# A top-2-of-8 expert layer at the end of a two-layer trunk: another deal of the small experts' chunks, expert outputs gated as soon as they are whole, two finishes side by side, and other costs in the planner's clock

## The chip, the cores and the metric

One core of one Trainium2 chip. The metric is the device time of the whole kernel in microseconds (us), median of several runs. Engines are named as in the profile: PE (TensorE) for matmuls and transpositions, PEld its weight loads, DVE (VectorE), ACT (ScalarE), POOL (GpSimd), SP (SyncE), which here only issues DMAs.

## The reference

256 latent tokens and 256 context tokens of width 1024 go through two layers. Layer 0 has a mixer (gated MLP over chunks, windowed attention, state-space scan) and a dense SwiGLU; layer 1 has a mixer and eight SwiGLU experts of which each token uses two. All is float32. What the change touches most is the expert layer:

```python
def swiglu(h, wg, wu, wd):
    return (jax.nn.silu(h @ wg) * (h @ wu)) @ wd

def moe_ffn(h, w_r, wg, wu, wd):
    logits = (h @ w_r).astype(jnp.float32)
    top_v, top_i = lax.top_k(logits, TOP_K)
    gates = jax.nn.softmax(top_v, axis=-1)
    combine = jnp.sum(jax.nn.one_hot(top_i, N_EXPERTS, dtype=jnp.float32) * gates[..., None], axis=-2).astype(h.dtype)
    out = jnp.zeros_like(h)
    for e in range(N_EXPERTS):
        out = out + combine[..., e:e + 1] * swiglu(h, wg[e], wu[e], wd[e])
    return out
...
        x = x + mod[5] * f
```

Each expert has gate and up weights of 1024 x 2816 and a down weight of 2816 x 1024; `mod[5]` is a row of 1024 factors.

## The kernel before

**Two stages.** Up to about 890 us the kernel does both mixers, layer 0's dense SwiGLU and the router (called the first stage below). From there to the end it does the experts (the expert stage), in which every one of 264 weight tiles of 1 MB comes from HBM once, in an order fixed when the program is built, on SP's queue.

**Experts by rank.** The router ranks the experts by the number of their tokens. Ranks 0, 1 and 2 are "wide" (128 token slots; rank 0 has 32 more, the "rest", `NE` in the code, that use its weights too), ranks 3, 4 and 5 have 64 slots, ranks 6 and 7 have 32 (`CAPS`). An expert's work goes in 11 chunks of 256 hidden columns, three tiles each: two of gate and up, one of down. A wide chunk needs its weights split in a high and a low part: ACT copies (`whi`, L275), DVE subtracts (`wlo`, L276), and PE makes three products. Small chunks use the raw float32 tile (`wraw`) at once, in row and column tiles of the array (`tiled` L1561, `tiled_up`).

**Order of the expert stage.** `RUNS` (L1530) says which small chunks go beside which wide expert: a run is a wide expert's 11 rounds with so many 32-slot and 64-slot chunks dealt among them. Before: four 32-slot chunks, then expert 1 with 6 of 32 and 11 of 64 slots, expert 0 with 6 and 11, expert 2 with 4 and 11, and two 32-slot chunks last. A round of `experts` (L1600) is on PE: gate and up of the wide chunk (`gu`, 24 matmuls of 512 columns), down of the previous wide chunk (`py`, 12), for expert 0 the same for the rest (`gux`, `pyx`), then gate/up (`gu`) and down (`pys`) of the small chunks, and the transpositions of the hidden rows (`mTx`, `mT`). For 32 slots the transposition is a matmul by `sel`, a sum of two permutations, which also adds the two halves (`turn`); ACT and DVE then make `silx` (`turned`, L1592 on).

**Finishes.** When an expert's down sums stand complete in PSUM, `finishes` (L1755) runs it through `finish` (L1762): DVE multiplies by `mod5row` (`y`, L1774 and L1778; for 32 slots in four pieces of 32 rows), ACT and DVE split it in `yh` and `yl`, PE scatters it back to tokens with a one-hot matrix (`ohT`, from `onehot` L1500) into `sc`, and DVE adds it with the token's gate to `acc` (L1788). One finish runs at a time, and `y` is made only when the one-hot is there. The finish that comes last sends out eight DMAs of 128x256 (L1791). `finish` is a generator that gives way after each unit, so its matmuls lie among those of the chunks.

**What sets the order.** In the expert stage the instructions of PE and ACT are in the order in which the program wrote them. Which generator steps next, and when splits and loads are laid, goes by a planner's clock (`clk`): every matmul (`mm`, L366) and transposition (`tp`, L381) adds its assumed cost to it, and `PIECE`, `LANDS` and `SPLIT` are the assumed times of a tile on the queue and of a split. `Weights._due` lets a wide tile be split when the clock has passed the tile's landing and the last split:

```python
        if not net.routed:
            return net.o.clk - self.at[i] > net.LAG
        return net.o.clk > self.land[i] and net.o.clk > self.splits - net.SPLIT / 2
```

In the first stage the same clock times the splits (`LAG`) and the generators, and a list scheduler orders the engines' streams from there. Raw tiles live in 12 buffers in the expert stage; a load is issued when a buffer comes free.

Of the kernel before, what the change touches and what calls it, by code (L numbers as in the profile page):

```python
# [340 lines left out]
class Net:  # L341
# [1158 lines left out]
    def onehot(self, p):  # L1500

        nc = self.nc
        yield from until(lambda: len(self.ohT) < 2)
# [10 lines left out]
        ohT = self.mp.tile([P, 2, P], F32R, tag="ohT", name="ohT", bufs=2)  # L1514
# [5 lines left out]
    YB, YH = 1, 1  # L1520
    NRAW, MKRAW = 4, 5
    MPRAW, HL_B, LAG, NS = 3, 2, 6.0, 2
    PIECE, LANDS, SPLIT = 2.45, 4.8, 1.15
# [4 lines left out]
    RUNS = ((None, (4, 0)), (1, (6, 11)), (0, (6, 11)), (2, (4, 11)), (None, (2, 0)))  # L1528
# [32 lines left out]
    def tiled(self, ps, x, w, ws, a, z):  # L1561

        m = x.shape[-1]
        n = (ws.stop - ws.start) * m // P
        for g in range(P // m):
            self.mm(ps[m * g:m * g + m, :n], x, w[:, ws.start + n * g:ws.start + n * g + n], a, z)
            if g:
                self.o.clk -= 4 * n * 0.000422

    def tiled_up(self, ps, x, w, k):  # L1570

        for g in range(2):
# [3 lines left out]
            if g or k % 2:  # L1576
                self.o.clk -= 4 * 256 * 0.000422

    def narrow_mid(self, ps, m):
        v = self.mp.tile([P, 256], F32, tag=f"mid{m}", name="mid", bufs=2 if m == 32 else 1)  # L1580
# [3 lines left out]
    def turn(self, pt, at, v, m):  # L1584
        for j in range(2):
            b = v[:, P * j:P * j + P]
            if m == 32:
                self.mm(pt[:, at + 64 * j:at + 64 * j + 64], b, self.sel, True, True)
            else:
                self.tp(pt[:, at + P * j:at + P * j + P], b)  # L1590

    def turned(self, pt, at, m):  # L1592

        src = pt[:, at:at + 4 * m].rearrange("p (j g s) -> p j g s", j=2, g=2)
# [5 lines left out]
    def experts(self):  # L1600
# [6 lines left out]
        self.finishing = False  # L1607
        self.ndone = 0
        self.sel = self.mp.tile([P, 64], F32, name="sel", bufs=1)
        nc.vector.tensor_tensor(self.sel, self.c("ident", 0, 64), self.c("swap", 0, 64), op=ALU.add)  # L1610
        o.spawn(self.gather(0), 2)
        pw, pn = None, []
        for w, ns in self.rounds() + [(None, [])]:
# [71 lines left out]
            if mids:  # L1685
                pt, at = self.bank("mTx"), 0
                for *_, m, v in mids:
                    self.turn(pt, at, v, m)
                    at += 4 * m
            pw = None  # L1690
            if w:
                pm = self.bank("mT")
                for j in range(2):
                    self.tp(pm[:, P * j:P * j + P], sil[:, P * j:P * j + P])
                mh = self.mp.tile([P, 256], F32R, tag="mh", name="mh", bufs=1)
                ml = self.mp.tile([P, 256], F32R, tag="ml", name="ml", bufs=1)
                self.split(mh, ml, pm[:, :256])
                pw = [*w, mh, ml, None]
            at = 0
            for p, c, m, v in mids:  # L1700
                mx = self.turned(pt, at, m)
                at += 4 * m
# [6 lines left out]
    def down(self, p, c, mh, ml):  # L1709
# [12 lines left out]
        if z and p:  # L1722
            self.o.spawn(self.finishes(p), 1)
        return w

    def down_rest(self, w, c, mx):
# [13 lines left out]
        if c == NCH - 1:  # L1740
            self.o.spawn(self.finishes(0), 1)

    def down_small(self, p, c, mx):
# [8 lines left out]
        if c == NCH - 1:  # L1752
            self.o.spawn(self.finishes(p), 1)

    def finishes(self, p):  # L1755
        yield from until(lambda: not self.finishing)
        self.finishing = True
        for q in (p, NE) if p == 0 else (p,):
            yield from self.finish(q)
        self.finishing = False  # L1760

    def finish(self, p):  # L1762
# [4 lines left out]
        w = 512 if m > 32 else 256  # L1767
        yield from until(lambda: self.ohT.get(p) is not None)
        ohT = self.ohT[p]
        for n in range(2 if m == P else 1):  # L1770
            yh, yl = (self.mp.tile([P, 512], F32R, tag=nm, name=nm, bufs=self.YH) for nm in ("yh", "yl"))
            y = self.mp.tile([P, 512], F32, tag="xsum", name="y", bufs=self.YB)
            if m == P:
                nc.vector.tensor_tensor(y, self.py[p][n], self.mod5row[:, 512 * n:512 * n + 512], op=ALU.mult)  # L1774
            else:
                for g in range(parts):
                    rows = slice(m * g, m * g + m)
                    nc.vector.tensor_tensor(y[rows, :w], self.py[p][rows, :w], self.mod5row[rows, w * g:w * g + w], op=ALU.mult)  # L1778
            self.split(yh[:, :w], yl[:, :w], y[:, :w])
            yield 3.0  # L1780
            for g in (n,) if m == P else range(parts):
                cs = slice(w * g, w * g + w)
                rows = slice(m * g, m * g + m) if parts > 1 else slice(0, P)
                for t in range(2):
                    pz = self.bank("sc")
                    for i, v in enumerate((yh, yl)):
                        self.mm(pz[:, :w], ohT[rows, t, :], v[rows, :w], i == 0, i == 1)
                    nc.vector.scalar_tensor_tensor(self.acc[:, t, cs], pz[:, :w], self.gate[:, t, p:p + 1], self.acc[:, t, cs],  # L1788
                                                   op0=ALU.mult, op1=ALU.add)
                    if self.ndone == NE:  # L1790
                        nc.sync.dma_start(self.out[P * t:P * t + P, cs], self.acc[:, t, cs])  # L1791
                    yield 1.0
        del self.ohT[p]
        self.ndone += 1

# [87 lines left out]
    def run(self):  # L1883
# [7 lines left out]
        with tc.tile_pool(name="keep", bufs=1) as keep, ExitStack() as self.pools, ExitStack() as self.kax, tc.tile_pool(name="sm", bufs=2) as self.sp, \  # L1891
                tc.tile_pool(name="w", bufs=2) as self.wp:
            self.const = keep.tile([P, NKEEP], F32, name="const")
            self.params = keep.tile([P, NPARAM], F32, name="params")
            self.csil = keep.tile([P, KB, 38], F32, name="csil")
            self.eps = keep.tile([P, 1], F32, name="eps")
            self.modT = [keep.tile([P, 48, 2], F32, name=f"modT{l}") for l in range(2)]
            self.wr = keep.tile([P, KB, NE], F32, name="wr")
            self.acoef = keep.tile([P, 16], F32, name="acoef")
            self.nsink = keep.tile([P, 16], F32, name="nsink")  # L1900
            nc.scalar.dma_start(self.csil, d["cT"])
            self.act_fn(self.csil, self.csil, AF.Silu)
            nc.scalar.dma_start(self.params, d["params"])
            nc.scalar.dma_start(self.const[:, :2 * P], d["consts"][:, :2 * P])
            nc.vector.memset(self.eps, EPS)
            self.act_fn(self.acoef, self.par("a_log"), AF.Exp)
            nc.vector.tensor_scalar(self.acoef, self.acoef, -1.0, None, op0=ALU.mult)
            nc.vector.tensor_scalar(self.nsink, self.par("sink"), -1.0, None, op0=ALU.mult)
            self.nb, self.nc_banks = 4, 3
            self.w = Weights(self, self.plan(), self.nraw, self.nhi)  # L1910
            with tc.tile_pool(name="psA", bufs=4, space=PSUM) as self.pp, tc.tile_pool(name="g", bufs=self.ng) as self.gp:
                self.ka = self.kax.enter_context(tc.tile_pool(name="keepA", bufs=1))
                self.gb = self.kax.enter_context(tc.tile_pool(name="act", bufs=2 * KB))
# [39 lines left out]
```

## Time and profile before

| | |
|---|---|
| device time, median of 3 runs | 1577.04 us (1576.43 to 1578.16) |
| device time of the profiled execution | 1578.03 us |
| span of the profiled execution | 1576.2 us |
| granted TensorE clock, mean | 0.981 |
| PE busy | 1495.8 us (95%) |
| DVE, ACT, POOL busy | 820.8, 666.9, 102.7 us |
| HBM read | 393.47 MB |

The profiled execution is 1.83 us longer than its span, and 0.99 us longer than the median. Read first the slices of the span (where PE and the DMA engines are busy), then windows of the expert stage, then the end.

### The profile page before, as it was taken

The page shows a single profiled execution, that of the slowest core. Times are in us where ns is not written, and L with a number is a line of the kernel's source. Part 1 is how long each engine was busy: PE and PEld are TensorE (multiplying, and loading weights), DVE is VectorE, ACT ScalarE, POOL GpSimd, SP SyncE. Part 2 cuts the span into 40 slices and gives each one's busy share as a digit, 9 for nine tenths or more (in the row PEclk, how much of TensorE's full clock was granted, in tenths as well). Part 3 has the DMA queues.
Part 4 walks back from the last instruction along what each step waited for, and adds up shares of the span by engine and source line. Part 5 has one row for each costly group of instructions (what it writes and reads, how often), then busy time and mean ns, then how long its engine had stood idle before and what let it go on. Part 6 is the DMA issues. An engine that isn't in the chain of part 4 may idle for free. (4 is left out here: it accounts for less than half of the span.)

```text
span 1576.2 us, 23531 instructions
## 1 busy us (share of the span) xinstructions
PE 1495.8 (95%) x9318; PEld 1077.2 (68%) x9319; DVE 820.8 (52%) x1481; ACT 666.9 (42%) x1189; POOL 102.7 (7%) x135
## 2 busy tenths in 40 slices
PE   4999998899999999999999999999899999999997
PEld 1766675787887787878747776666566666656654
DVE  2687568553333333478775344544465444654545
ACT  3566644343222212356565354444343443433541
POOL 1200123210000000030310000000000000000000
PEclk8999999999999999999999899999999999999998
DMA  9422055432324333234164599999998999999994
GB/s 374 152 107 108 8 211 204 154 133 88 154 81 160 133 107 114 101 135 161 54 260 178 181 406 419 419 419 420 417 397 358 374 410 417 419 408 410 419 420 164
DMA packets 57715, 396.10 MB, mean 251 GB/s; under 512 B 6528, under 2 KB 8576, under 8 KB 10496
## 3 DMA queue, kind: packets, MB, share of 16 engines
q1 hardware_dynamic: 56016, 392.03, 62.5%
q10 hardware_dynamic: 1584, 2.52, 0.5%
q8 instruction: 75, 1.23, 0.3%
q14 instruction: 40, 0.33, 0.1%
HBM read 393.47 MB, written 1.05 MB: 250 GB/s over the span
## 5 line engine op out<-in xcount | busy, mean ns | idle before, releaser
L276 DVE TENSOR_TENSOR wlo<-wraw,whi 128x1024 fp32r<-128x1024 f32 (+2 forms) x318 | 377.0, 1222 | 161.3 <-ACT whi L275 156.0
L275 ACT ACTIVATE whi<-wraw 128x1024 fp32r<-128x1024 f32 (+2 forms) x318 | 320.0, 1047 | 148.4 <-PE fd L374 57.9
L374 PE MATMUL gu<-whi,xw 128*128 128x512 f32 x528 | 167.5, 398 | 4.2 <-ACT whi L275 4.2
L374 PE MATMUL gu<-wraw,xs 128*64 128x256 f32 (+1 forms) x1760 | 168.5, 392 | 0.5 <-ACT xs L1492 0.5
L374 PEld LDWEIGHTS gu<-wraw,xs 128*64 128x64 f32 (+1 forms) x1760 | 95.0, 128 | 65.3 <-issue 16.4
L374 PEld LDWEIGHTS gu<-whi,xw 128*128 128x128 f32 x528 | 95.9, 188 | 24.4 <-ACT whi L275 6.2
L374 PE MATMUL gu<-wlo,xw 128*128 128x512 f32 x264 | 104.3, 395 | 3.5 <-DVE wlo L276 3.5
L1167 DVE TENSOR_TENSOR fsil<-fsil,fu 128x512 f32<-128x512 f32 x22 | 15.1, 688 | 153.5 <-PE fu L374 118.2
L374 PE MATMUL pys<-wraw,silx 128*32 128x256 f32 (+1 forms) x616 | 87.7, 480 | 6.8 <-DVE y L1778 4.1
L430 ACT ACTIVATE fsil<-fg 128x512 f32<-128x512 f32 x22 | 13.1, 598 | 174.3 <-PE fg L374 174.3
L1581 ACT ACTIVATE mid<-gu 128x256 f32<-128x256 f32 x55 | 21.0, 382 | 139.8 <-PE gu L374 139.8
L374 PE MATMUL fg<-ahi,whi 128*128 128x512 f32 (+1 forms) x192 | 72.3, 377 | 0.0
L374 PE MATMUL fg<-alo,whi 128*128 128x512 f32 (+1 forms) x192 | 71.6, 373 | 0.3 <-POOL alo L528 0.3
L374 PE MATMUL fg<-ahi,wlo 128*128 128x512 f32 (+1 forms) x192 | 71.4, 372 | 0.0
L374 PE MATMUL fu<-alo,whi 128*128 128x512 f32 (+1 forms) x192 | 71.4, 372 | 0.0
L374 PE MATMUL fu<-ahi,wlo 128*128 128x512 f32 (+1 forms) x192 | 71.3, 372 | 0.0
L374 PE MATMUL fu<-ahi,whi 128*128 128x512 f32 (+1 forms) x192 | 71.3, 372 | 0.0
L374 PE MATMUL fd<-mhi,whi 128*128 128x512 f32 (+1 forms) x188 | 70.7, 376 | 0.0
L374 PE MATMUL fd<-mhi,wlo 128*128 128x512 f32 (+1 forms) x188 | 70.6, 375 | 0.0
L374 PE MATMUL fd<-mlo,whi 128*128 128x512 f32 (+1 forms) x188 | 70.6, 375 | 0.0
L374 PE MATMUL modp<-wraw,csil 128*32 128x512 f32 x384 | 55.5, 615 | 12.8 <-ACT csil L430 7.4
L374 PEld LDWEIGHTS gu<-wlo,xw 128*128 128x128 f32 x264 | 49.5, 188 | 18.0 <-DVE wlo L276 7.4
(346 smaller groups left out, 2824.8 us busy)
## 6 DMA issues: line engine op xcount, KB each, us to landing
wraw<-in_moe_dram SPq DMA_DIRECT2D x264, 1024.0 KB, 12.6
wraw<-in_wmod_dram SPq DMA_DIRECT2D x48, 1024.0 KB, 6.4
wraw<-in_fgu_dram SPq DMA_DIRECT2D x22, 1024.0 KB, 4.8
wraw<-in_win_dram SPq DMA_DIRECT2D x16, 1024.0 KB, 4.9
wraw<-in_wout_dram SPq DMA_DIRECT2D x8, 1024.0 KB, 6.4
wraw<-in_fdn_dram SPq DMA_DIRECT2D x8, 1024.0 KB, 6.4
wraw<-in_fdn_dram SPq DMA_DIRECT2D x4, 768.0 KB, 4.9
wraw<-in_wgd_dram SPq DMA_DIRECT2D x2, 1056.0 KB, 4.9
```

Of the source, the lines that this page charges most:

```text
L275: nc.scalar.activation(hi[:, cs], t[:, cs], AF.Copy)
L276: nc.vector.tensor_tensor(lo[:, cs], t[:, cs], hi[:, cs].bitcast(F32), op=ALU.subtract)
L374: self.nc.tensor.matmul(out, l, r, start=start, stop=stop)
L430: self.last_act = self.nc.scalar.activation(out, in_, func, **kw)
L1167: self.nc.vector.tensor_tensor(s, s, pu, op=ALU.mult)
L1581: self.nc.scalar.activation(v, ps[:, :256], AF.Copy)
```

## The change

- **Deal.** `RUNS` becomes: four 32-slot chunks first (as before), expert 1 with 2 of 32 and 14 of 64 slots, expert 0 with 10 and 5, expert 2 with 2 and 14, four 32-slot chunks last.
- **Turns.** The 32-slot turn is two transpositions instead of two matmuls by `sel`; the sum of halves that `sel` made is now an ACT copy (`sum32`) and a DVE addition. Two turns share a bank.
- **Gates early.** `halves` (y, yh, yl) runs right after the last down matmul of an expert (`finished`); a wide expert's halves lie in a buffer of the `xw` ring (`fin`). A wide and a narrow finish may run at the same time. For 32 slots y is one operation on 128 rows (`mod5part`, four POOL copies made once).
- **Last finish.** For the expert that ends last, the 16 scatter matmuls go token half by token half in four row groups into four banks; DVE adds the first token half to `acc`, ACT and POOL the second; four DMAs of 128x512 on two queues.
- **Clock.** Other assumed costs in `mm`, `tp`, `tiled`, `tiled_up`, `PIECE`, `SPLIT`.
- **Room.** Small constants move to a pool that closes after the first stage.

```diff
-        f = 1 if (l.dtype == F32R and n >= 256) else 4
-        self.o.clk += f * max(n, 64) * 0.000422 + 0.002
+        if l.dtype == F32R and n >= 256:
+            self.o.clk += n * self.COL + 0.0135
+        else:
+            self.o.clk += max(0.22, 4 * n * self.COL + 0.008)
...
     def tp(self, out, src, n=P):
-        self.o.clk += 0.11
+        self.o.clk += 0.19
...
-        yield from until(lambda: len(self.ohT) < 2)
+        yield from until(lambda: len(self.ohT) < 3)
...
-    PIECE, LANDS, SPLIT = 2.45, 4.8, 1.15
+    PIECE, LANDS, SPLIT = 2.5, 4.8, 1.2
...
-    RUNS = ((None, (4, 0)), (1, (6, 11)), (0, (6, 11)), (2, (4, 11)), (None, (2, 0)))
+    RUNS = ((None, (4, 0)), (1, (2, 14)), (0, (10, 5)), (2, (2, 14)), (None, (4, 0)))
...
         for j in range(2):
-            b = v[:, P * j:P * j + P]
-            if m == 32:
-                self.mm(pt[:, at + 64 * j:at + 64 * j + 64], b, self.sel, True, True)
-            else:
-                self.tp(pt[:, at + P * j:at + P * j + P], b)
+            self.tp(pt[:, at + P * j:at + P * j + P], v[:, P * j:P * j + P])
...
+        if m == 32:
+            v = src.rearrange("p (j r c) -> p j r c", j=2, r=2)
+            src = self.mp.tile([P, 2, 64], F32, tag="sum32", name="sum32", bufs=1)
+            self.nc.scalar.activation(src, v[:, :, 0, :], AF.Copy)
+            self.nc.vector.tensor_tensor(src, src, v[:, :, 1, :], op=ALU.add)
...
+    def begin(self, p):
+        self.finishing[self.wide(p)] = True
+        return self.halves(p)
+
+    def finished(self, p):
+
+        self.o.wait(lambda: not self.finishing[self.wide(p)])
+        self.o.spawn(self.finishes(p), 1)
+        self.o.poll()
...
+        yield max(3.0, self.w.splits - self.o.clk + 3.0)
         yield from until(lambda: self.ohT.get(p) is not None)
...
+        if p == self.last:
+            yield from until(lambda: self.ndone == NE)
+            pz = [self.bank("sc") if g % 2 else self.pp.tile([P, 512], F32, tag="gu", name="scl", bufs=2) for g in range(4)]
+            for t in range(2):
+                for i, v in enumerate(ys[0]):
+                    for g in range(4):
+                        rows = slice(m * g, m * g + m)
+                        self.mm(pz[g][:, w * t:w * t + w], ohT[rows, t, :], v[rows, :w], i == 0, i == 1)
+            for g in range(4):
+                for t in range(2):
+                    cs, z = slice(w * g, w * g + w), pz[g][:, w * t:w * t + w]
+                    if t == 0:
+                        nc.vector.scalar_tensor_tensor(self.acc[:, t, cs], z, self.gate[:, t, p:p + 1], self.acc[:, t, cs],
+                                                       op0=ALU.mult, op1=ALU.add)
+                    else:
+                        v = self.mp.tile([P, 256], F32, tag=f"mid{32 if g % 2 else 64}", name="part", bufs=2)
+                        nc.scalar.activation(v, z, AF.Copy, scale=self.gate[:, t, p:p + 1])
+                        nc.gpsimd.tensor_tensor(self.acc[:, t, cs], self.acc[:, t, cs], v, op=ALU.add)
+                    if g % 2:
+                        cs = slice(w * (g - 1), w * g + w)
+                        (nc.scalar if t else nc.sync).dma_start(self.out[P * t:P * t + P, cs], self.acc[:, t, cs])
+            return
```

ACT in layer 0's mixer, at the norms of the gated MLP (`nl`, `ne`) and of the scan (`rs_l`, `rs_e`), before:

```order
L430 ACTIVATE nl<-nv 128x8
L430 ACTIVATE ne<-nl 128x8
L275 ACTIVATE whi<-wraw 128x1024
L442 ACTIVATE ahi<-att 128x512
L275 ACTIVATE whi<-wraw 128x1024
L1135 ACTIVATE gsq<-ysb 128x512 x2
L403 ACTIVATE rs_v<-gss,eps 128x512
L430 ACTIVATE rs_l<-rs_v 128x512
L430 ACTIVATE rs_e<-rs_l 128x512
```

The same place in the change:

```order
L1137 ACTIVATE gsq<-ysb 128x512 x2
L275 ACTIVATE whi<-wraw 128x1024 x2
L432 ACT_TABLE_LOAD
L432 ACTIVATE nl<-nv 128x8
L405 ACTIVATE rs_v<-gss,eps 128x512
L432 ACT_TABLE_LOAD
L432 ACTIVATE ne<-nl 128x8
L432 ACT_TABLE_LOAD
L432 ACTIVATE rs_l<-rs_v 128x512
L432 ACT_TABLE_LOAD
L432 ACTIVATE rs_e<-rs_l 128x512
```

The second `nl` and `ne` now come after `gsq` instead of before it, and every logarithm (`nl`, `rs_l`) and exponential (`ne`, `rs_e`) has a table load ahead of it; in the whole program ACT has 40 table loads instead of 28, the 12 more all in layer 0.

PE at the end of the expert stage, before (`gu` and `pys` of 32x256 are chunks of expert 6; the `sc` behind them are the finishes of experts 2, 5 and, at 128x256, 6):

```order
L374 MATMUL gu<-wraw,xs_8736 32x256 x8
L374 MATMUL pys<-wraw,silx 32x256 x8
L374 MATMUL mTx<-sel,mid 128x64 x2
L374 MATMUL pys<-wraw,silx 32x256 x8
L374 MATMUL sc<-yh,ohT 128x512
L374 MATMUL sc<-yl,ohT 128x512
...
L384 MATMUL ohT<-const,oh_12681 128x128 x2
...
L374 MATMUL sc<-yh,ohT 128x256
L374 MATMUL sc<-yl,ohT 128x256
```

The end in the change:

```order
L376 MATMUL sc<-yh,ohT 128x512
L376 MATMUL sc<-yl,ohT 128x512
L376 MATMUL pys<-wraw,silx 32x256 x8
L386 MATMUL mT<-const,mid 128x128 x2
L376 MATMUL gu<-wraw,xs_8720 32x256 x16
L376 MATMUL pys<-wraw,silx 32x256 x8
L386 MATMUL mT<-const,mid 128x128 x2
L376 MATMUL pys<-wraw,silx 32x256 x8
L386 MATMUL ohT<-const,oh_12753 128x128 x2
L376 MATMUL scl<-yh,ohT 128x256
L376 MATMUL sc<-yh,ohT 128x256
```

Before, 14 pairs of `sc` stand behind the last `pys` (2 of expert 2, 4 of expert 5, 8 of expert 6); now the scatters of experts 2 and 5 stand ahead of the last small chunk, and only the 16 matmuls of the last expert come behind.

## Rows read from the trace of the kernel before

**Rows 1.** The page, 40 slices of 39.4 us: DMA share in tenths, GB/s.

```profile
DMA  9422055432324333234164599999998999999994
GB/s 374 152 107 108 8 211 204 154 133 88 154 81 160 133 107 114 101 135 161 54 260 178 181 406 419 419 419 420 417 397 358 374 410 417 419 408 410 419 420 164
```

**Rows 2.** Windows: us, busy us of PE, PEld, DVE, ACT, POOL, clock, DMA share, GB/s.

```profile
920.00:1117.00 197.00, 190.18 (x1269) 127.70 (x1268) 89.69 (x114) 87.75 (x146) 0.00 (x0) 1.00 1.01 417
1117.00:1347.00 230.00, 226.15 (x1822) 148.71 (x1823) 118.06 (x164) 97.97 (x163) 0.00 (x0) 1.00 0.97 395
1347.00:1540.00 193.00, 184.55 (x1132) 118.42 (x1130) 103.25 (x134) 81.34 (x123) 0.00 (x0) 0.99 1.01 415
1540.00:1550.00 10.00, 9.53 (x83) 5.36 (x80) 4.53 (x9) 2.27 (x7) 0.00 (x0) 1.00 0.95 394
1550.00:1560.00 10.00, 8.48 (x85) 4.76 (x86) 6.24 (x11) 2.48 (x6) 0.00 (x0) 1.00 0.02 7
```

**Rows 3.** Groups by form on PE, 900 to 1550 us: busy us, mean ns, idle before.

```profile
L374 PE MATMUL gu<-wraw,xs 128*64 128x256 f32 x1056 | 122.3, 383 | 0.0
...
L374 PE MATMUL pys<-wraw,silx 128*64 128x512 f32 x264 | 64.4, 609 | 4.1 <-DVE y L1778 4.1
...
L374 PE MATMUL gu<-wraw,xs 128*32 128x256 f32 x640 | 40.9, 394 | 0.0
L374 PE MATMUL pys<-wraw,silx 128*32 128x256 f32 x320 | 21.3, 384 | 2.0 <-DVE silx L1597 2.0
...
L374 PE MATMUL mTx<-sel,mid 128*128 128x64 f32 x124 | 19.5, 288 | 0.5 <-ACT mid L1581 0.5
L384 PE MATMUL mTx<-const,mid 128*128 128x128 f32 x66 | 13.4, 284 | 0.5 <-ACT mid L1581 0.5
```

**Rows 4.** The chain that ended last, its end: start, us, engine, operation.

```profile
1555.75 1.07 PE pys L374 x16
...
1563.98 0.44 DVE y L1778
...
1564.52 0.42 ACT yh L442
...
1569.34 0.80 PE sc L374 x2
...
1570.17 0.91 DVE acc L1788 x2
```

**Rows 5.** Groups by form on POOL, whole span.

```profile
L528 POOL TENSOR_TENSOR alo<-nu,ahi 128x256 fp32r<-128x256 f32 x24 | 22.0, 923 | 41.1 <-ACT nu L527 41.1
```

**Rows 6.** DMA issues, 1565 to 1577 us: count, KB each, us to landing.

```profile
out_dram<-acc SPq DMA_DIRECT2D x8, 128.0 KB, 1.9
```

**Rows 7.** Timeline of ACT, layer 0's mixer: start, us.

```profile
230.98 1.28 ACT L430 ACT_TABLE_LOAD   x1
232.28 0.63 ACT L430 ACTIVATE z<-z 128x512 f32<-128x512 f32 x1
...
249.35 0.21 ACT L430 ACTIVATE ne<-nl 128x8 f32<-128x8 f32 x1
...
251.88 1.14 ACT L1135 ACTIVATE gsq<-ysb 128x512 f32<-128x512 f32 x2
```

**Rows 8.** Windows of layer 0, columns as in rows 2.

```profile
230.00:240.00 10.00, 10.00 (x101) 5.84 (x103) 5.88 (x14) 6.39 (x9) 3.75 (x4) 1.00 0.62 221
240.00:250.00 10.00, 5.36 (x60) 3.71 (x54) 9.33 (x22) 6.33 (x13) 4.65 (x4) 0.98 0.97 406
250.00:260.00 10.00, 7.44 (x39) 4.61 (x36) 8.11 (x14) 4.96 (x8) 4.27 (x2) 0.85 0.16 39
300.00:320.00 20.00, 16.95 (x135) 14.62 (x134) 15.54 (x31) 12.69 (x27) 4.88 (x6) 1.00 0.40 158
```

**Rows 9.** Timeline of PE, then of POOL, at the gated MLP of layer 0.

```profile
257.51 1.09 PE L374 MATMUL gs<-gws,gv 128*64 128x128 f32 x16 [2.56 <-POOL gv L954]
...
254.21 3.25 POOL L954 TENSOR_TENSOR gv<-gv,gvg 128x512 f32<-128x512 f32 x1 [5.15 <-DVE gv L952]
```

More of the change, by code (lines that the diff above doesn't have):

```diff
@@ L1722, in down @@
         if z and p:
-            self.o.spawn(self.finishes(p), 1)
+            self.finished(p)
         return w
@@ L1752, in down_small, with halves, finish @@
         if c == NCH - 1:
-            self.o.spawn(self.finishes(p), 1)
-    def finishes(self, p):
[L1756 to L1762, printed above, removed]
+            self.finished(p)
+    def halves(self, p):
+        nc, m = self.nc, self.slots(p)
+        w = 512 if m > 32 else 256
+        if m == P:
+            f = self.mp.tile([P, 2, KB, P], F32R, tag="xw", name="fin", bufs=2).rearrange("p a k s -> p (a k s)")
+            ys = [(f[:, 1024 * n:1024 * n + 512], f[:, 1024 * n + 512:1024 * n + 1024]) for n in range(2)]
+        else:
+            ys = [tuple(self.mp.tile([P, 512], F32R, tag=nm, name=nm, bufs=1) for nm in ("yh", "yl"))]
+        for n, (yh, yl) in enumerate(ys):
+            y = self.mp.tile([P, 512], F32, tag="xsum", name="y", bufs=self.YB)
+            if m == P:
+                nc.vector.tensor_tensor(y, self.py[p][n], self.mod5row[:, 512 * n:512 * n + 512], op=ALU.mult)
+            else:
+                if m == 32:
+                    nc.vector.tensor_tensor(y[:, :w], self.py[p][:, :w], self.mod5part, op=ALU.mult)
+                else:
+                    for g in range(2):
+                        rows = slice(m * g, m * g + m)
+                        nc.vector.tensor_tensor(y[rows, :w], self.py[p][rows, :w], self.mod5row[rows, w * g:w * g + w], op=ALU.mult)
+            self.split(yh[:, :w], yl[:, :w], y[:, :w])
+        return ys
+    def finishes(self, p):
+        yield from self.finish(p, self.begin(p))
+        if p == 0:
+            yield from until(lambda: not self.finishing[False])
+            yield from self.finish(NE, self.begin(NE))
+    def begin(self, p):
[5 more added lines that the diff above has]
+        self.o.poll()
+    def finish(self, p, ys):
         nc = self.nc
@@ L1767, in finish @@
         w = 512 if m > 32 else 256
+        wide = m == P
+        yield max(3.0, self.w.splits - self.o.clk + 3.0)
         yield from until(lambda: self.ohT.get(p) is not None)
         ohT = self.ohT[p]
[L1770 to L1783, printed above, removed]
-                for t in range(2):
[L1785 to L1792, printed above, removed]
@@ new lines, in finish @@
+        for g in range(D // w):
+            cs = slice(w * g, w * g + w)
+            rows = slice(0, P) if wide else slice(m * g, m * g + m)
+            for t in range(2):
+                pz = self.bank("sc")
+                for i, v in enumerate(ys[g if wide else 0]):
+                    self.mm(pz[:, :w], ohT[rows, t, :], v[rows, :w], i == 0, i == 1)
+                    self.o.clk += 0.11
+                nc.vector.scalar_tensor_tensor(self.acc[:, t, cs], pz[:, :w], self.gate[:, t, p:p + 1], self.acc[:, t, cs],
+                                               op0=ALU.mult, op1=ALU.add)
+                yield 1.0
@@ L1793, in finish @@
         del self.ohT[p]
         self.ndone += 1
+        self.finishing[wide] = False
     def overflow(self):
```

88 lines of the change are left out of this document (48 added, 40 removed).

## The prediction

> **What bounds the kernel now.** I read the slices of the span first. From slice 23 on the DMA engines stand at nine tenths and 419 GB/s, so the expert stage goes at the pace of its weight tiles: 1 MB (1.049 million bytes) at 419 GB/s is 2.50 us. Slices 29 to 31 fall to 397, 358 and 374 GB/s [rows 1]; there something else sets the pace. Then windows, one for each wide expert's run. In expert 1's run (920 to 1117) and expert 2's (1347 to 1540) the queue moves 417 and 415 GB/s and PE is busy 190.18 of 197 and 184.55 of 193 us. In expert 0's run (1117 to 1347) it moves 395 GB/s and PE is busy 226.15 of 230 [rows 2]: 28 chunks need 84 tiles, 84 x 2.50 = 210 us of queue, but PE needs 226. Buffers come free too late, and the queue loses 230 x (1 - 395/419) = 13 us. Last the end: 394 GB/s in 1540 to 1550 puts the last byte at about 1549.4 (9.4 of the 10 us), and in 1550 to 1560 there is next to nothing [rows 2]. The span ends at 1576.2, so 26.8 us pass after the last byte: the last small chunks and then 14 pairs of `sc` with a DVE addition each, in the chain's last rows one after the other [rows 4].
>
> So there are three things to price: PE's surplus in expert 0's run, the 26.8 us of tail, and what the first stage does under another order.
>
> **The deal.** By PE's groups of the expert stage a 64-slot chunk costs (122.3 + 64.4 + 13.4)/33 = 6.07 us and a 32-slot chunk 40.9/20 + 21.3/20 + 19.5/31 = 3.74 us [rows 3]. These are busy times, some tenths over the true spacing. A turn by transpositions (13.4/33 = 0.41) in place of one by `sel` (19.5/31 = 0.63) gives 0.22 us per 32-slot turn.
>
> - Expert 0's run gets 4 more of 32 and 6 fewer of 64 slots, and 21 cheaper turns (10 chunks, 11 of the rest): 226.2 + 4 x 3.74 - 6 x 6.07 - 21 x 0.22 = 200 us. One 64-slot expert now ends inside expert 1's run, with its finish and the next one's gather; I put that at 4 us (four pairs of `sc` at 0.80 [rows 4], the rest a guess). PE needs 196; the queue has 26 chunks x 3 x 2.50 = 195. Twelve raw buffers are 30 us of lead, which covers a difference of a few us.
> - Expert 1's run: 190.2 + 3 x 6.07 - 4 x 3.74 + 4 = 197 against 27 x 7.5 = 202.5. Expert 2's: 184.6 + 3 x 6.07 - 2 x 3.74 = 195 against 202.5. Both stay under the queue.
>
> So of the 13 us I take 11 as gained. Bounds: nothing (the dips move to another run), and 15 (all of it, and some of the 415 and 417 GB/s). I take nearly all since every run now needs PE no longer than the queue.
>
> The extra ACT copy and DVE addition of 33 turns lie on engines that are half idle (820.8 and 666.9 of 1576.2 us busy); I cost them at nothing. Their cover is that the last chunk's gate and up tiles land 2.5 us before its down tile; without it they cost some 0.5 us once.
>
> **The tail.** At the end are now four 32-slot chunks: 12 tiles, 30 us of queue, against 4 x 3.52 = 14 us of PE. The finishes of experts 2 and 5 (8 pairs, some 9 us) fit between. Behind the last byte stand: the last `pys` 1.07, y 0.44, yh 0.42, yl about as long, gaps 0.2, together 2.55; 16 `sc` matmuls; additions; output. Of the matmuls a pair takes 0.80 [rows 4], so 6.4 us one after another and 1.7 if four groups run fully side by side; I take 3.0, nearer to side by side, since the chain's pair also holds its start after a wait. For the additions, ACT's scaled copy is like yh (0.42), POOL's addition has its nearest row in `alo`, 0.92 for 128x256 [rows 5]; four of them after the first copy are 4.1 us, and DVE's four at 0.46 lie beside them. From the last addition (1571.08) to the span's end is 5.1 us now, with one DMA landing in 1.9 [rows 6]; fewer and larger DMAs on two queues I leave at 5.1. Sum 14.8 instead of 26.8: minus 12. Bounds: 11.5 (1.7 for the matmuls, half of the POOL additions under them) to 19 (6.4, and all the rest), so minus 15 to minus 8.
>
> The Trainium skill, page "TensorE: Matmul & The Clock Gate", section "Measured speedup vs the span model", has four row groups at 3.07 times the speed of one; by that the 16 matmuls would take an estimated 2.1 us and the sum would be 0.9 us lower. No row of this trace shows four row groups into four banks, so 3.0 stays.
>
> **The first stage.** ACT gets 12 more table loads, all in layer 0. One takes 1.28 us, and the next activation starts 0.02 us behind it [rows 7]: 15.4 us in all. What of it counts depends on the place. Three stand at `gu` and `seg`, where PE is busy 10.00 of 10 us [rows 8]: hidden. The next five (`nl`, `ne`, `rs_l`, `rs_e`) lie where PE has only 5.36 and 7.44 of 10 [rows 8], in the chain of the gated MLP and the scan's norm: the second `nl` and `ne` now come after `gsq`, two splits and two loads, so `ne` ends near 258.8 instead of 249.6 [rows 7] (251.9 + 1.1 + 2.1 + 1.3 + 0.2 + 0.7 + 1.3 + 0.2). POOL's `gv` (3.25) follows and `gs` waits for it (2.56 us of PE idle, at 257.51) [rows 9]; `gs` moves to about 262.5, 5 us later, and the gated MLP's rows of the output projection with it. Then norm 2: two loads between `rs_v` and `rs_e`, 2.6 us, and PE idles there already (16.95 of 20 busy) [rows 8], so they count. The last two come when PE is busy with the SwiGLU; I give them and the changes around the router 0.4. Sum plus 8. Bounds: all 15.4 of the loads; and minus 2, since the scheduler's new order can also pack better (layer 1 has its last attention matmuls sooner).
>
> **Sum.** Profiled execution 1578.0 - 11 - 12 + 8 = 1563.0. The median lies 1.0 below the profiled execution: **1562.0**, faster by about 15.
>
> The early gates free the PSUM banks of `pys` sooner: PE waited 4.1 us for `y` once [rows 3]. That wait is inside expert 0's run and already in its 13.
>
> **Rivals.**
>
> - *First stage hides it* (the chains have slack that I don't see): loads cost 0 to 2: 1555. For it: PE is busy nearly throughout layer 0; against: the idle windows lie just where the loads go. Chance 0.15.
> - *Dips move.* In expert 1's and 2's runs, a wide chunk takes PE some 9.2 us (190.2 less 11 x 6.07 and 6 x 3.74, over 11), a round with two 64-slot chunks 9.2 + 12.1 = 21.3 us for nine tiles (22.5), and finishes come on top; if buffers again come free late, the 11 us stay lost: 1573. For it: 195 to 197 of 202.5 is close to full; against: 30 us of lead. Chance 0.15.
> - *PE late at the end*: run 2 leaves PE behind, the last chunks wait for it and the tail gives only 4: 1570. Chance 0.05.
> - *Gates in front of splits: slower.* ACT and DVE take their work in order. `halves` now puts y in DVE's stream where PE's last down matmul is still to come, with yh on ACT and yl on DVE behind it; splits of the next wide tile stand behind those, and PE waits for the splits. A price is the 4.1 us that PE once waited around a y [rows 3]. There are nine finishes; eight such stalls more, on PE in runs with no slack, are 33 us: 1595. It is slower than before from the fourth or fifth stall on. Against it: after `py` the next PE work is small chunks of raw tiles, which need no split. Chance 0.07.
> - *Loads that hold ACT twice as long: slower.* If each load kept ACT for another 1.28 us and all 12 were on the path, it were 12 x 2.57 = 31 us in place of 8: 1585. Rows 7 show the next activation 0.02 us behind the load. Chance 0.03. The Trainium skill, "ScalarE: Activation LUTs", section "What ACT_TABLE_LOAD costs", speaks against the change in this way: a load of about 1283 ns and a drain of about 1380 ns, 2.66 us for each switch, 31.9 us for twelve. The load agrees with the trace, the drain does not appear in it.
>
> **How the numbers follow.** Forecast 0.55, with its own range 1554 to 1569 (bounds of the tail, half of the first stage's). A measurement here tells 0.2% (3.2 us) from no change, so faster means below 1573.9. Faster: 0.55 + 0.15 + 0.05 and half of the dips, 0.07: 0.82. Same: 0.08. Slower: 0.10. The range for 8 in 10 leaves out the two slower cases and a little below: 1551 to 1574.
>
> **What would show it.** Right: windows of expert 0's run at 415 GB/s or more; last byte some 3 us earlier on the clock of the span (minus 11, plus 8); 15 us from there to the end; first expert chunk 8 us later; PE idle at `gs` near 262 and at norm 2. Wrong: 395 GB/s in another run, DVE or ACT idle behind y for some us at each finish, an expert stage that starts no later than before, or more than 20 us after the last byte.

## The result, and the profile after

The change is slower: 1588.68 us (median of 6, 1583.85 to 1591.41) against 1576.95 us before (median of 6, 1576.43 to 1578.16). The ratio is 1.0071, 95% interval 1.0057 to 1.0084. The forecast was 1562, with 1551 to 1574 as range; the measured time lies outside it, on the other side of before. The profiled execution took 1586.61 us, its span is 1584.6 us, 8.4 more than before.

The slices of the changed kernel (columns as in [rows 1]):

```profile
DMA  9422045233323322342334689999989999999996
GB/s 367 156 102 112 30 158 226 90 123 133 144 96 148 144 101 89 129 161 80 134 133 160 239 351 419 419 416 419 418 345 419 416 382 418 419 410 385 419 419 268
```

Slices count from 0. From slice 24 on the queue is at its 419 GB/s, one slice later than before, and the dips did not go: slices 29, 32 and 36 have 345, 382 and 385 GB/s, where [rows 1] has its lowest, 397, 358 and 374, in slices 29 to 31. Slice 36 lies in expert 2's run, which had no such dip before.

The gather of the first expert (`xe`), the first row of the expert stage on PE in the changed kernel:

```profile
908.91 0.38 PE L376 MATMUL xe<-oh,hr 128*128 128x32 f32 x2 [0.78 <-DVE cnt L1394]
```

Before it started at 891.37 us, so the first stage ends 17.5 us later. The windows of the expert stage, columns as in [rows 2] (expert 1's run, expert 0's, expert 2's, then the end):

```profile
938.00:1134.00 196.00, 190.31 (x1180) 131.36 (x1179) 99.79 (x125) 92.92 (x149) 0.00 (x0) 0.98 1.01 419
1134.00:1338.00 204.00, 198.99 (x1734) 132.90 (x1733) 112.14 (x171) 97.87 (x176) 0.00 (x0) 1.00 0.96 397
1338.00:1540.00 202.00, 195.09 (x1178) 130.18 (x1182) 106.00 (x141) 85.75 (x133) 0.00 (x0) 0.98 1.00 411
1540.00:1560.00 20.00, 17.70 (x174) 7.87 (x166) 11.10 (x20) 4.21 (x11) 0.00 (x0) 1.00 1.01 417
1560.00:1570.00 10.00, 5.33 (x60) 2.00 (x52) 0.80 (x3) 1.20 (x5) 0.00 (x0) 0.82 0.78 324
1570.00:1584.00 14.00, 4.03 (x34) 1.90 (x34) 2.74 (x7) 2.65 (x7) 2.81 (x4) 0.50 0.22 80
```

Expert 0's run is shorter (204 us with 78 tiles dealt to it, instead of 229 with 84; a run lasts from its wide expert's first `gu` to the next one's), and the queue still moves no more than 397 GB/s in it (395 in [rows 2]). By these rates it loses 204 x (1 - 397/419) = 11 us there instead of 13, and in expert 2's run 4 us instead of 2. The last byte lands near 1567.7 (324 of 419 GB/s in 1560 to 1570), and 16.9 us follow it instead of 26.8.

So the 8.4 us of the span split in three: first stage plus 17.5; from the first gather to the last byte 658.8 us instead of 658.0, plus 0.8; tail minus 9.9. The forecasts were plus 8, minus 11 and minus 12. The last byte is an estimate from the rates of windows. If the landing of the last weight tile is taken in its place (1551.6 before, 1569.1 in the change), the split is plus 17.5, 0.0 and minus 9.1. Either way the middle stretch did not get shorter.

### The profile page after: what moved, and what is told of

The parts are those of the page before. It is cut to its first block, busy times and chain, and to the rows that moved or that the text cites. A ratio compares the mean times of both kernels' runs of the same rounds, so it can differ in the third digit from the quotient of the medians.

```text
span 1584.6 us, 23465 instructions
## 1 busy us (share of the span) xinstructions
PE 1486.5 (94%) x9252; PEld 1077.5 (68%) x9253; DVE 822.2 (52%) x1500; ACT 694.1 (44%) x1238; POOL 103.7 (7%) x143
## 4 chain that ended last, share of the span: by engine, by line
PE 76%; DVE 9%; DMA 5%; ACT 5%; issue 3%; POOL 1%; ACTq 0%; POOLq 0%; DVEq 0%; SPq 0%
PE gu L376 18%; PE fg L376 8%; PE fu L376 8%; PE fd L376 8%; PE py L376 5%; PE pys L376 4%; DMA wraw<-in_moe_dram 4%; PE op L376 3%; DVE wlo L276 3%; PE modp L376 2%; PE xbcp L376 2%; PE S L376 1%; PE gvp L376 1%; PE xe L376 1%; PE gux L376 1%
## 5 line engine op out<-in xcount | busy, mean ns | idle before, releaser
L432 ACT ACTIVATE fsil<-fg 128x512 f32<-128x512 f32 x22 | 13.2, 598 | 173.7 <-PE fg L376 173.7
```

What stands on the lines that cost most here:

```text
L432: self.last_act = self.nc.scalar.activation(out, in_, func, **kw)
```

## Where the first stage lost 17.5 us

The chain of the changed kernel in layer 0's gated MLP and scan norm (start, us, what; "ACT L432" without a tile is a table load):

```profile
255.75 3.42 PE gss L376 x4
...
259.19 0.69 ACT rs_v L405
...
259.90 1.28 ACT L432
...
261.19 0.21 ACT ne L432
...
261.42 1.28 ACT L432
...
263.37 1.28 ACT L432
...
265.32 0.69 DVE rs_l L408
...
266.76 1.59 POOL gv L956
...
268.39 1.14 PE gs L376 x8
```

The exponential `ne` (261.19) stands behind `rs_v` (259.19) in ACT's order, and `rs_v` waits for PE's `gss`, which runs at 0.86 us a matmul here (0.54 before) and ends at 259.2. Three loads follow, and DVE's and POOL's `gv` come behind them, since DVE first takes `rs_l`, which needs the loads too. `gs` starts at 268.4 instead of 257.5 [rows 9]: 10.9 us late. At norm 2, two loads lie between `rs_v` and `rs_e` on the same chain:

```profile
312.00 0.49 ACT rs_v L405
...
312.55 1.28 ACT L432
313.85 0.42 ACT rs_l L432
...
315.63 0.42 ACT rs_e L432
...
323.28 0.21 PE fg L376
```

`rs_v` comes 9.5 us late here (302.5 before), and `rs_e` ends 12.0 late (304.0 before). `fg`, the SwiGLU's first product, has its first matmul at 322.9 instead of 310.1. By the trace the first layer's SwiGLU ends 14.6 us late, and the first gather starts 17.5 late. The next activation starts 0.01 to 0.02 us behind each load of these chains; a drain, as the Trainium skill has it ("ScalarE: Activation LUTs", "What ACT_TABLE_LOAD costs"), does not appear here either.

Where ten of the 12 loads come from can be read in the code and the trace. `act_fn` notes in `self.table` which function the program wrote last, and before a logarithm or an exponential it loads, if need be, the table set that has both (`load_table`, L438 before, L440 in the change). The note follows the order in which the program wrote the instructions, not the one that the list scheduler makes of it. ACT's last such load ahead of these norms, before and then in the change, and in the change what follows it:

```profile
234.07 1.28 ACT L438 ACT_TABLE_LOAD   x1
```

```profile
227.69 1.28 ACT L440 ACT_TABLE_LOAD   x1
...
241.85 1.28 ACT L432 ACT_TABLE_LOAD   x1
243.15 1.15 ACT L432 ACTIVATE z<-z 128x512 f32<-128x512 f32 x2
```

Before, the `z` of [rows 7], a Silu, is done when the joint set comes (234.07), and no load is needed for any `nl`, `ne`, `rs_l` or `rs_e` until norm 2 is over. In the change `z` comes behind the joint set and brings its own (241.85); the program believes the joint set still there, and from then on each logarithm and each exponential of these norms has a load of its own (six up to 264 us, four at norm 2). The other two loads come from `gu`, also a Silu, between the exponentials of `seg`. No run tests the joint load by itself.

PE's granted clock was lower here as well. Windows of the changed kernel, columns as in [rows 8]:

```profile
250.00:260.00 10.00, 7.54 (x28) 4.02 (x28) 8.39 (x12) 7.01 (x11) 1.84 (x2) 0.66 0.65 258
320.00:330.00 10.00, 8.79 (x46) 8.21 (x47) 5.76 (x14) 7.00 (x12) 2.40 (x3) 0.66 0.37 147
```

Before, the clock was 0.85 in the first of them [rows 8] and 1.00 in the second. What the clock adds to the 17.5 us is not isolated by any run.

## The experiments

Ratios are to the kernel before on the same chip, with the 95% interval. The planner's costs until the routing are called the first stage's costs.

**e1_old_clock_first_stage, e2_new_clock_first_stage, e4_old_deal, e7_old_clock_all.** E1 is the change with the old costs in the first stage. This brings back the old order on ACT and PE, instruction for instruction up to 855 us; a few instructions around the router still differ. E2 is the kernel before with the new costs in the first stage.

```diff
+        if not self.routed:
+            f = 1 if (l.dtype == F32R and n >= 256) else 4
+            self.o.clk += f * max(n, 64) * 0.000422 + 0.002
+        elif l.dtype == F32R and n >= 256:
...
-        self.o.clk += 0.19
+        self.o.clk += 0.19 if self.routed else 0.11
```

> The change, but with the planner's old costs until the routing: ACT has the 28 table loads of before, and the instructions of PE and ACT in the first stage are those of before; the expert stage's PE order is that of the change. Theory A (the clock's costs in the first stage cost 17 us by order and table loads, nothing else does): first expert gather back at 891 us (909 in the change, 891 before), time 1588.7 - 17.5 = 1571 us, faster than before by 6. Rival B (the late start only shifts slack that the expert stage had anyway, the queue sets the end): gather at 891, but the end no earlier than 1580.

Measured: 1570.53 us, ratio 0.9956 (0.9942 to 0.9970).

> The kernel before, with the new costs only until the routing: ACT has 40 table loads, first stage in the change's order, expert stage as before. Theory A: gather at 909, time 1577 + 17.5 = 1594.5 us. Rival B: 1577 to 1582, since the queue fills its buffers while the router works and sets the end anyway.

Measured: 1594.96 us, ratio 1.0114 (1.0093 to 1.0135). The first gathers on PE, in the first kernel and then in the second:

```profile
891.62 0.38 PE L380 MATMUL xe<-oh,hr 128*128 128x32 f32 x2 [0.78 <-DVE cnt L1398]
```

```profile
909.44 2.88 PE L380 MATMUL xe<-oh,hr 128*128 128x32 f32 x21 [0.78 <-DVE cnt L1398]
```

Theory A holds in both directions: 891.6 and 909.4, and by the ratios the times move by 18 us each way (1.0071 to 0.9956, 1 to 1.0114). The costs in the clock, meant for the place of splits, cost 18 us by the order that they give the first stage.

E4 is e1 with the old line of `RUNS`; e7 is the change with all costs old.

> As the first of these kernels (old costs until the routing), with the old deal of small chunks in runs (6 and 11, 6 and 11, 4 and 11, two last). Theory A (the deal shortens expert 0's run by 20 us, and its dips of the queue go): slower than the first kernel by about 10 us, 1581, with 395 GB/s in expert 0's run. Rival C (dips move, the deal is worth nothing): within 3 us of the first kernel.

Measured: 1577.33 us, 0.9992 (0.9978 to 1.0006): 0.0036 above e1, some 6 us. The deal helps, by about half of what was expected; neither the 10 us of theory A nor rival C's zero. In e4's trace expert 0's run takes 236 us, against 229 with the same deal before the change, so these 6 us are a gain over a run that the other parts of the change had made longer.

> The change with the planner's old costs in both stages, all else as in the change. Theory A (only the first stage's order matters): as the first kernel, 1571 within 3 us. Rival D (the new costs also place the splits better in the expert stage, and the gain there comes from them): 1577 to 1582, and PE waits more for high and low parts.

Measured: 1579.98 us, 1.0019 (1.0006 to 1.0033): 0.0063 above e1, 10 us. Rival D: in the expert stage the new costs are worth having. PE's waits for the low parts of the weights from 900 to 1545 us (in all, times, longest), in e7 and then in e1:

```profile
PE gu L374 <- DVE wlo L276: 11.2, 16, 1.7
```

```profile
PE gu L380 <- DVE wlo L276: 2.0, 2, 1.5
```

With the old costs PE waits for a split in 16 places, with the new ones in two.

**e9_costs_alone.** The kernel before with the new costs in the expert stage alone.

```diff
+        if not self.routed:
...
+        elif l.dtype == F32R and n >= 256:
+            self.o.clk += n * self.COL + 0.0135
...
-    PIECE, LANDS, SPLIT = 2.45, 4.8, 1.15
+    COL = 0.000417
+    PIECE, LANDS, SPLIT = 2.5, 4.8, 1.2
```

> The kernel before with the new costs in the expert stage alone (nothing else of the change). Theory I (the new costs place splits better, whatever the deal): faster than before by 6 to 10, 1567 to 1571. Rival J (they only help with the new deal and turns): within 3 us of before.

Measured: 1582.27 us, 1.0018 (1.0003 to 1.0033). Rival J: without the rest of the change they gain nothing.

**e5_late_gates, e8_old_last_finish.** e1 with the finishes made late and one at a time, and e1 with the old last finish.

```diff
-        self.o.wait(lambda: not self.finishing[self.wide(p)])
         self.o.spawn(self.finishes(p), 1)
-        self.o.poll()
...
-        if p == self.last:
...
+                if self.ndone == NE:
+                    nc.sync.dma_start(self.out[P * t:P * t + P, cs], self.acc[:, t, cs])
```

> As the first kernel (old costs until the routing, 1570.5), with the finishes as before: y, yh, yl made when the one-hot is there, one finish at a time; the last finish in four row groups stays. Theory E (gates at once and finishes side by side put waits of PE behind DVE and ACT, 3.0 us for acc and 2.5 us for sum, and let the clock fall behind them: they cost what deal and costs gain): faster than the first kernel by 6 to 12, 1559 to 1565. Rival F (early gates free the banks and cost nothing): 1570 to 1576.

Measured: 1569.51 us, 0.9941 (0.9921 to 0.9961). Theory E falls: 2 us better than e1, with intervals that overlap. The early gates neither cost nor gave anything that shows here.

> As the first kernel, with the last finish as before: pairs of sc with a DVE addition each, eight DMAs of 128x256; early gates stay. Both theories: the time from the last byte to the end was 26.8 us before and is 17.6 in the first kernel; if the four row groups give it, it grows by 4 to 7 us, 1575 to 1577.5; if the earlier finishes of the other two experts give it, it stays within 2 us.

Measured: 1573.95 us, 0.9952 (0.9931 to 0.9973), as e1. In e8's trace 17.6 us follow the last byte (175 GB/s in 1550 to 1560 put it at 1554.2, the span ends at 1571.8), as in e1. The four row groups and POOL's help are not what shortened the tail. What is left is that the scatters of experts 2 and 5 no longer stand behind the last `pys`: before, they ran from 1556.8 to 1562.3 there.

**e13_less_rest.** e1 with part of expert 0's rest left out.

```diff
-                for k in range(KB):
+                for k in range(2):
                     self.tiled_up(px, self.xe[NE], held[k // 4], k)
+                self.o.clk += 0.48 * 3
```

> As the first kernel, with 12 of the 16 gate/up matmuls of expert 0's rest left out in each of its 11 rounds (that part of the result is not computed); all other work, loads and their order stay. PE has 11 x 1.4 = 15.8 us less to do in expert 0's run. Theory K (PE sets the pace of that run even with the new deal: its 205 us against 195 of the queue, and full buffers are no slack for a late PE): expert 0's run falls to about 195, the queue moves over 410 GB/s in it, and the time falls by 8 to 12 against the first kernel. Rival N (splits on ACT and DVE hold the buffers): within 3 us of the first kernel, GB/s as there.

Measured: 1562.34 us, 0.9890 (0.9867 to 0.9913): 0.0066 under e1, 10 us. Windows of experts 1, 0 and 2, first of e1, then of this kernel:

```profile
920.00:1117.00 197.00, 191.28 (x1184) 132.14 (x1184) 99.64 (x125) 92.34 (x149) 0.00 (x0) 0.99 1.01 416
1117.00:1322.00 205.00, 200.04 (x1730) 133.76 (x1729) 111.68 (x170) 97.79 (x176) 0.00 (x0) 0.99 0.96 394
1322.00:1530.00 208.00, 201.08 (x1232) 132.46 (x1230) 108.80 (x145) 87.03 (x135) 0.00 (x0) 0.98 1.00 412
```

```profile
920.00:1120.00 200.00, 193.38 (x1203) 133.66 (x1204) 101.75 (x127) 95.50 (x152) 0.00 (x0) 0.98 1.01 416
1120.00:1314.00 194.00, 187.13 (x1472) 125.43 (x1470) 112.20 (x171) 97.60 (x176) 0.00 (x0) 0.99 0.99 409
1314.00:1530.00 216.00, 207.49 (x1289) 135.15 (x1287) 113.83 (x155) 88.97 (x140) 0.00 (x0) 0.98 1.01 417
```

The outer ends, 920 and 1530, are the same in both and are no ends of a run; the middle window is expert 0's run. It falls from 205 to 194 us and its queue rises from 394 to 409 GB/s. PE is busy 12.9 us less in it (200.04 to 187.13), and 10 us come off the time. Theory K holds: even with the new deal PE sets the pace of that run, and most of what is taken from PE there comes off the time.

**e6_sel_turn, e10_sel_turn_late_gates, e11_sel_turn_at_ends, e12_sel_at_ends_late_gates.** The 32-slot turn by `sel`, in e1, in e5, and at the two ends of the expert stage only (`sel` true for all 32-slot turns, or for the first and last four chunks; in e6 and e10 the line reads `if m == 32`).

```diff
+            if sel:
+                self.mm(pt[:, at + 64 * j:at + 64 * j + 64], b, self.sel, True, True)
+            else:
+                self.tp(pt[:, at + P * j:at + P * j + P], b)
```

> As the first kernel, with the 32-slot turn as the matmul by sel again (no copy on ACT, no addition on DVE), in the new pairs of a bank. Theory G (copy and addition lie in front of the splits on ACT and DVE and lengthen the way from gate/up to down): faster than the first kernel by 4 to 10. Rival H (they are hidden, and the transpositions save PE 0.22 us in each of 33 turns): slower by 4 to 7.

Measured: 1565.70 us, 0.9911 (0.9892 to 0.9930): 7 us under e1, as theory G has it.

> As the first kernel (old costs until the routing, 6.9 under before), with both the turn by sel (13.4 under before when alone) and the late gates, one finish at a time (9.6 under before when alone). If the two add: 15 to 17 under before, some 1561. If both mend the same waits (the finishes at the ends of runs): 12 to 14 under, 1564.

Measured: 1570.41 us, 0.9951 (0.9934 to 0.9969): a miss for both; no better than e5, and 6 us above e6, from which only the late gates set it apart. So with the turn by `sel` the early gates would be worth 6 us, and with transpositions nothing (e5 against e1).

> As the first kernel, with the turn by sel for the first four and the last four 32-slot chunks alone (there no wide expert's work lies between), transpositions in the rounds; the sum of halves is written into the chunk's own buffer. Theory L (copy and addition cost where a chunk's turn is waited for, four times 0.6 us at the start and some at the end, and the transpositions do save PE 0.2 to 0.4 us a turn in the rounds): at least as fast as sel everywhere, 13 to 17 under before. Rival M (copy and addition cost in the rounds, in ACT's and DVE's streams): 7 to 10 under before.

Measured: 1569.58 us, 0.9943 (0.9924 to 0.9961). Theory L falls, rival M's band holds the time.

> The kernel just before with late gates too. Theory L: 15 to 19 under before, the best of all; rival M: 9 to 12 under.

Measured: 1569.61 us, 0.9935 (0.9910 to 0.9959): likewise rival M's. Part of the disagreement of e6 and e10 goes with the granted clock of their runs: at a mean clock of 0.983 to 0.984 two runs of each took 1564.5 to 1565.7 us, and seven runs of e10 at 0.975 to 0.981 took 1567.8 to 1574.5. Since e6 and e10 disagree by more than their intervals, the turn's cost was measured in another way.

**e14_triple_sum.** e1 with the turn's copy and addition made three times.

```diff
+            for _ in range(2):
+                self.nc.scalar.activation(src, v[:, :, 0, :], AF.Copy)
+                self.nc.vector.tensor_tensor(src, src, v[:, :, 1, :], op=ALU.add)
```

> As the first kernel (old costs until the routing), with ACT's copy and DVE's addition of every 32-slot turn made three times instead of once (the result is the same, PE's order too). If copy and addition cost what the first run without them suggested (7 us for 33 turns): 12 to 16 us slower than the first kernel. If they are hidden but for the start and the end: 2 to 6 us slower. If they cost nothing at all: within 2 us.

Measured: 1597.75 us, 1.0106 (1.0089 to 1.0123): 0.0150 above e1, 24 us for two more. PE's waits in the expert stage (in all, times, longest), of e1 and then of this kernel, and a window of this kernel that holds most of expert 0's run (1127 to 1349):

```profile
PE pys L380 <- DVE silx L1608: 4.4, 3, 2.8
...
PE py L380 <- ACT whi L275: 0.7, 1, 0.7
```

```profile
PE pys L380 <- DVE silx L1611: 8.9, 5, 4.1
PE py L380 <- ACT whi L275: 7.6, 10, 1.3
```

```profile
1120.00:1330.00 210.00, 195.12 (x1625) 126.95 (x1622) 116.78 (x196) 102.21 (x204) 0.00 (x0) 0.98 0.91 367
```

`pys` waits longer for `silx`, and `py` waits 7.6 us in ten places for `whi`, where e1 has one such wait of 0.7 us: the copies stand in front of splits on ACT. The queue falls to 367 GB/s over 210 us of which PE is busy 195. The two extra pairs are not hidden; they cost more than the 12 to 16 us foreseen.

**e15_early_deal, e16_early_deal_sel_turn.** e1 with the deal rounded up, so that small chunks come early in a run; then with the turn by `sel` as well.

```diff
-                ns = [q.pop(0) for q, m in zip(small, counts) for _ in range(m * (i + 1) // n - m * i // n)]
+                ns = [q.pop(0) for q, m in zip(small, counts) for _ in range(-(-m * (i + 1) // n) + (-m * i // n))]
```

> As the first kernel, with the deal of each run rounded up, so that small chunks come in a run's early rounds (expert 0's run: 1 of 32 and 1 of 64 slots in its first round, none in its last). Theory O (the queue loses 6 us between 1120 and 1160 since two rounds there have 6 and 5 tiles for 32 us of PE while the buffers are full): that dip goes, 3 to 6 us faster than the first kernel. Rival P (PE's sum over the run is all that counts, and the dip moves into the run's end): within 2 us.

Measured: 1568.14 us, 0.9938 (0.9922 to 0.9953), 2 to 3 us under e1 with intervals that overlap. Its windows:

```profile
1120.00:1180.00 60.00, 58.23 (x452) 37.48 (x454) 33.38 (x49) 26.65 (x46) 0.00 (x0) 1.00 0.88 350
1180.00:1330.00 150.00, 148.13 (x1340) 100.03 (x1333) 81.29 (x125) 74.44 (x135) 0.00 (x0) 1.00 1.00 410
```

The dip at the start of expert 0's run stays (350 GB/s over the 60 us from 1120 on, where e1 has 373). Theory O falls.

> As the kernel just before, with the 32-slot turn by sel everywhere. If the turn's copy and addition cost much: 5 to 8 us faster than the kernel just before, and the fastest of all, 16 or more under before; if not: within 3 us of it.

Measured: 1561.57 us, 0.9900 (0.9883 to 0.9917): 6 us under e15, and the fastest of the kernels that compute the whole result. This is not the change with two parts taken back, since the early deal is new in it; that kernel is e6, 14 us faster than the kernel before, and its interval overlaps with e16's.

## Why the prediction was wrong, step by step

Three terms make up the miss. Against the profiled execution the first stage is off by 9.5 us (plus 17.5 for plus 8), the middle stretch by 11.8 (plus 0.8 for minus 11) and the tail by 2.1: 1563.0 + 23.4 = 1586.4, and 1586.61 was measured. The median then lies 2.1 above the profiled execution, not 1.0 below it as before.

- **The first stage, plus 8: mis-sized.** The place was right (`gs`, norm 2), the sum was not. It had "so `ne` ends near 258.8", adding ACT's own durations from `gsq` on. It left out that `rs_v`, which stands ahead of `ne` on ACT, waits for PE's `gss`: `ne` ended at 261.4, and DVE took `rs_l` before `gv`. `gs` came 10.9 us late, not 5. Norm 2 was as priced (9.5 late before its loads, 12.0 behind them). "I give them and the changes around the router 0.4" measured 5.5, the rest up to the first gather; no run takes that part to pieces. In all 17.5, above even the upper bound of 15.4, which counted loads and neither reordering nor clock. E1 and e2 show it both ways.
- **The deal, minus 11: the size of PE's work and the cover were wrong.** PE was to need 196 us in expert 0's run; it was busy 199 of 204, against 195 of queue. Moreover "Twelve raw buffers are 30 us of lead, which covers a difference of a few us" has it the wrong way round. At the start of expert 0's run (1134.3 us) 96 weight tiles have landed and 101 loads have been issued, so 89 tiles are used up and all 12 buffers are taken; from 1160.8 to 1168.0 no tile lands. Full buffers are cover for a late transfer, none for a late PE. So a late round of PE costs the queue soon, as the rival "dips move" had it; most of the loss stayed in that same run (11 us), and 2 us moved to expert 2's. The deal gives 6 us by e4, but not against the kernel before, where the stretch shows no gain at all; e13 shows that PE paces the run. One detail was wrong too: I counted a gather with the moved finish. The three 64-slot experts are gathered together ahead of expert 1's run (from 918 before, from 937 in the change), so none moved with it.
- **The extra copy and addition "at nothing": wrong.** They are on the way from gate/up to down and in front of the splits. In e14 two more pairs cost 24 us. One pair in place of `sel` costs about 6 to 7 by e6 and e16, but e10 against e5 shows none, so its size stays open between 0 and 7.
- **The tail, minus 12: nearly right** (minus 9.9), in part by luck, since its terms are off both ways. Forecast and measured: from the last byte to the scatters 2.55 and 6.2, scatters 3.0 and 1.5, additions 4.1 and 5.0, output 5.1 and 4.3. (The upper bound adds up to 18.2 and not to 19.) The rows of the changed kernel's end:

```profile
1566.77 1.93 PE L376 MATMUL pys<-wraw,silx 128*32 128x256 f32 x16 [1.52 <-DMA wraw<-in_moe_dram]
1568.64 0.69 PE L386 MATMUL mT<-const,mid 128*128 128x128 f32 x2
1569.36 0.28 ACT L1597 ACTIVATE sum<-mT 128x128 f32<-128x128 f32 x1 [3.66 <-PE mT L386]
...
1570.56 1.94 PE L376 MATMUL pys<-wraw,silx 128*32 128x256 f32 x16 [1.24 <-DVE silx L1604]
...
1573.90 0.58 PE L376 MATMUL scl<-yh,ohT 32*128 32x256 f32 x1 [0.78 <-ACT yh L444]
...
1574.96 0.41 PE L376 MATMUL sc<-yl,ohT 32*128 32x256 f32 x1
...
1576.54 1.40 POOL L1830 TENSOR_TENSOR acc<-acc,part 128x256 f32<-128x256 f32 x2 [670.13 <-ACT part L1829]
...
1577.97 0.36 ACTq L1833 DMA_DIRECT2D out_dram<-acc  x1
1578.38 0.47 ACT L1829 ACTIVATE part<-scl,gate 128x256 f32<-128x256 f32 x1 [1.59 <-POOL acc L1830]
...
1578.93 1.40 POOL L1830 TENSOR_TENSOR acc<-acc,part 128x256 f32<-128x256 f32 x2 [0.99 <-ACT part L1829]
```

  The 16 matmuls took 1.5 us (1573.90 to 1575.37), not 3.0; the estimate from the Trainium skill's page ("TensorE: Matmul & The Clock Gate", "Measured speedup vs the span model") was 2.1. But the last chunk's turn stands behind the `pys` of the chunk before it, which waits for its own tile, so the copy, the addition and a second `pys` of 1.94 (at a granted clock of 0.50; [rows 4] has 1.07) came after the last byte. And ACT's output DMA waits for POOL's additions, with ACT's third copy queued behind it: 1.6 us of waiting at 1578.38. I had priced four additions as one stream.
- **The rival "gates in front of splits"**: e5 shows no such cost. It named the right side of the result, the wrong mechanism. The wait that priced it, and that the prediction puts "inside expert 0's run", lies in expert 2's, which begins at 1346.6 in the kernel before:

```profile
1382.71 3.63 PE L374 MATMUL pys<-wraw,silx 128*64 128x512 f32 x8 [4.13 <-DVE y L1778]
```

- **The costs in the expert stage** had no term at all. They are worth 10 us with the new deal (e7), and nothing without it (e9).

Not settled: how much of the effects of deal, turn, early gates and costs hangs on each other, what offset the 11 us of the deal, and the size of the turn. One kernel's runs differ by some us among themselves, which is the size of these effects.

## What to carry to other kernels

A planner's cost that sets the order in two stages must be tested in each alone: here it gains 10 us in one, beside the other parts, and loses 18 in the other. A note of an engine's state that is kept in program order, as `self.table` is, goes stale when a scheduler reorders that engine. When an instruction is moved, follow everything that now stands ahead of it on its engine, with the wait of each, and not just their durations. A ring of buffers that is full covers late transfers only; where the producer is ahead, most of what is taken off the consumer's work comes off the time (10 of 12.9 us in e13).

## What the runs showed of the hardware

The granted clock fell after two short waits of PE in the middle of the expert stage. In the changed kernel PE waits 3 us for a split (first row), and the window from 1040 to 1060 has a mean of 0.83, part of it at the lower level of 1.2 GHz:

```profile
1044.84 1.22 PE L376 MATMUL gu<-whi,xw 128*128 128x512 f32 x2 [3.04 <-ACT whi L275]
```

```profile
1020.00:1040.00 20.00, 18.35 (x138) 12.69 (x137) 6.75 (x10) 6.60 (x15) 0.00 (x0) 1.00 1.01 419
1040.00:1060.00 20.00, 16.92 (x93) 10.79 (x93) 10.97 (x15) 10.84 (x17) 0.00 (x0) 0.83 1.01 413
```

The matmul pair takes 1.22 us there, and 0.63 in the rounds at full clock. A wait of 3.00 us that ends at 1358.85 is followed by the same (0.83 in 1350 to 1370), while a wait of 2.53 us that ends at 1263.53 is not (1.00 in 1260 to 1280).

The time of a kernel's runs goes with their mean clock. The six runs of the changed kernel lie between 1583.85 us at 0.975 and 1591.41 us at 0.967. The kernel before does the same: in its 26 runs measured together with e1's the fastest took 1573.73 us at 0.988, and the slowest 1581.82 us at 0.980. So a few us between two medians can be a difference of clocks, and the spread is not a mark of the change.
